# Layer 0 of a two-layer diffusion trunk: when the attention heads' rows are turned, and where the experts' row numbers are made

## The chip, the cores and the metric

The kernel runs on one core of a Trainium2 chip. The metric is the device time of one execution in microseconds, the median of several runs. All work is in 32-bit floating point. The core's engines each take their instructions in a fixed order and wait for one another by semaphores: TensorE multiplies matrices into PSUM (eight banks), VectorE, ScalarE and GpSimd do elementwise work, and the queues of SyncE, ScalarE and GpSimd issue transfers.

## The reference, cut to what matters

There are 256 latent tokens and 256 context tokens of width 1024. Layer 0 normalises them, projects them to five groups of 512 columns (u, gate, q, k, v), runs a recurrence (RG-LRU, in two directions) over u and neighbourhood attention over q, k, v, projects both results back, and then runs a mixture of 16 experts. Layer 1 has other mixers and the same experts. The two parts that the change touches are these:

```python
ux, ug, q, k, v = _split(h @ w_in, EVEN_SPLITS)
...
q, k, kc = rms_norm(q, q_g), rms_norm(k, k_g), rms_norm(kc, k_g)   # per head of 64 columns
...
top_v, top_i = lax.top_k(e_logits, MOE_TOP_K)                      # two experts for each token
...
for e in range(MOE_EXPERTS):
    hid = jax.nn.silu(t @ w1[e]) * (t @ w3[e])
    out = out + gate[:, e:e + 1] * (hid @ w2[e])
```

## The kernel before, in words

**Who sets the order.** The program is written with a framework that tracks the dependencies. Its planner gives each engine its order when the program is built: it reckons with its own costs when each instruction's inputs are ready, and of those that are ready it takes the one that stands earliest in the program. The chip then keeps that order, whether the costs were right or not. PSUM banks have tags: four of tag "a" (results of projections), three of tag "b" (short-lived results), one of tag "m". The buffers of one tag are handed out in turn, so the fourth "b" result waits until the first has been read. The context manager `in_order(PE)` ties TensorE's instructions within it to the order of the program.

**Weights.** A stream of 1 MB pieces comes from memory. `chunk` hands out 1024 columns at a time; each chunk is split by `split` into a rounded part (`L339`, ScalarE) and a rest (`L342`, mostly VectorE, some on GpSimd), with four buffers of each kind, and `mm3` does three matmuls for each product (`L348` to `L350`).

**Projections of layer 0.** `proj` runs a projection in four steps, each of one chunk and 24 matmuls, and yields after each. `qk_rows(0)` projects q: after its four steps it copies the four banks of 128 tokens out (`L698`), squares (`L700`), sums by head (`L701`), computes the reciprocal root (`L704`, `rsqrt`), and yields. Then, for each of the four groups of tokens t, it scales the rows (`L709`, VectorE), transposes them with four TensorE transposes into a "b" bank (`L713`), and writes them to `qT` or `kT` (`L716`, ScalarE). `qk_rows(1)` does the same for k, and then v and the gate are projected. `weave` runs these as its main line, and after each yield of it one and a half steps of the recurrence `lru` (gates `L659` to `L668`, then a root `L670` and scans `L672` to `L684`, once for each direction) and one step of the modulation (`L437`).

**Experts of layer 0.** For each expert e: `first` multiplies the gathered tokens by w1 and w3 (24 matmuls each), `second` by w2 (24 matmuls), `hidden` transposes the result between them (`L1589`), and `take` transposes the next expert's tokens (`L1558`). `rows` makes the list of an expert's tokens two experts ahead: a one-hot matrix (`L1507`, VectorE), four small matmuls for the row numbers into one "b" bank (`L1543`), the row numbers (`L1546`), the gather, then four small matmuls for the gates into a second "b" bank (`L1550`) and their sum (`L1551`). The loop runs p1 of e, `hidden(e-1)`, `take(e+1)`, `rows(e+2)`, p3 of e, `second(e-1)`.

Of the kernel before, what the change touches and what calls it, by code (L numbers as in the profile page):

```python
# [13 lines left out]
OP = mybir.AluOpType  # L14
AX = mybir.AxisListType
PE = mybir.EngineType.PE
# [3 lines left out]
D = 1024  # L20
KC = 8
EPS = 1e-6
NE = 16
# [194 lines left out]
def run_all(g):  # L218
    for _ in g:
        pass  # L220
# [8 lines left out]
NP = 2  # L229
# [23 lines left out]
class Trunk:  # L253
# [361 lines left out]
    def even(self, xn):  # L615
        nc, I, F, R = self.nc, self.I, self.F, self.R
        enter = self.enter(0, xn)
        next(enter)
        hT = self.hT
# [72 lines left out]
        def qk_rows(which):  # L692
            banks = [self.bank("a") for _ in range(4)]
            yield from self.proj([("row", banks[t], t, 0, 512) for t in range(4)], hT)
            ss, rs, rows = F.get(4, 8), F.get(4, 8), [nr() for _ in range(4)]
            jr = Ring(F, 1, 512)
            for t in range(4):
                nc.scalar.copy(rows[t], banks[t])  # L698
                j = jr()
                nc.scalar.activation(j, rows[t], AF.Square)  # L700
                nc.vector.tensor_reduce(ss[:, t], j.rearrange("p (h d) -> p h d", h=8), AX.X, OP.add)  # L701
            F.free(jr)
            ssf, rsf = ss.rearrange("p a b -> p (a b)"), rs.rearrange("p a b -> p (a b)")
            nc.vector.tensor_scalar(ssf, ssf, 1.0 / 64, EPS, op0=OP.mult, op1=OP.add)  # L704
            self.rsqrt(rsf, ssf, 32)
            yield
            for t in range(4):
                qn = rows[t].rearrange("p (h d) -> p h d", h=8)
                nc.vector.tensor_tensor(qn, qn, rs[:, t].rearrange("p (h o) -> p h o", o=1).to_broadcast([P, 8, 64]),  # L709
                                        op=OP.mult)  # L710
                tp = self.bank()
                for c in range(4):
                    nc.tensor.transpose(tp[:, c * P:(c + 1) * P], rows[t][:, c * P:(c + 1) * P], self.ident)  # L713
                tv = tp.rearrange("p (c t) -> p c t", c=4)
                ts_ = slice(t * P, (t + 1) * P)
                nc.scalar.activation((kT if which else qT)[:, :, ts_], tv, AF.Copy, scale=self.col("kg" if which else "qg"))  # L716
            F.free(ss, rs)
            yield

        def mains():  # L720
            yield from qk_rows(0)
            yield from qk_rows(1)
            banks = [self.bank("a") for _ in range(4)]
            yield from self.proj([("row", banks[t], t, 0, 512) for t in range(4)], hT)
            self.vr = F.get(4, 512)
            for t in range(4):
                nc.scalar.copy(self.vr[:, t], banks[t])
            self.ugb = [self.bank("a") for _ in range(4)]
            yield from self.proj([("ws", self.ugb[c], c, 0, 512) for c in range(4)], hT)
# [3 lines left out]
        vr, banks = self.vr, self.ugb  # L733
# [12 lines left out]
        gt = Ring(F, 2, 512)  # L746
        R.free(*hT)
        mh, ml = R.get(KC, 512), R.get(KC, 512)
        for c in range(4):
            t = gt()  # L750
# [769 lines left out]
    def experts_rows(self, l, nt, hd, rk, G, VAL, mxi):  # L1520


        nc, I, F, R = self.nc, self.I, self.F, self.R
# [3 lines left out]
        xgR, uR, yR = self.xgR, Ring(F, 2, 512), Ring(F, 2, D)  # L1527
# [9 lines left out]
        def rows(e):  # L1537

            oh = ohR()
            self.one_hot(oh, "iota", rk, e)  # L1540
            tb = self.bank()
            for t in range(nt):
                nc.tensor.matmul(tb[:, 0:2], oh[:, t], self.vi[:, t], start=(t == 0), stop=(t == nt - 1))  # L1543
            ohs[e] = oh
            gt, dst, xg = gtR(), ddR(), xgR()
            nc.vector.tensor_scalar(dst, tb[:, 0:1], tb[:, 1:2], BIG, op0=OP.add, op1=OP.add)  # L1546
            self.gather(hd, xg, dst)
            tg = self.bank()
            for t in range(nt):
                nc.tensor.matmul(tg[:, 0:3], oh[:, t], VAL[:, t, e], start=(t == 0), stop=(t == nt - 1))  # L1550
            nc.vector.tensor_reduce(gt, tg[:, 0:3], AX.X, OP.add)  # L1551
            st[e] = xg, gt, dst

        def turn(b, xg):
# [6 lines left out]
        def take(e):  # L1561

            xh, xl = xs[e] = xhR(), xlR()
            for b in range(2):
                ps = turn(b, st[e][0])
                pv = ps.rearrange("p (k t) -> p k t", k=4)
                nc.scalar.copy(xh[:, 4 * b:4 * b + 4], pv)
                nc.vector.tensor_tensor(xl[:, 4 * b:4 * b + 4], pv, xh[:, 4 * b:4 * b + 4].bitcast(F32),
                                        op=OP.subtract)

        def first(e):

            p1, p3 = self.bank("a"), self.bank("a")
            run_all(self.proj([("row", p1, 0, 0, 512)], xs[e]))
            u = uR()
            nc.scalar.activation(u, p1, AF.Tanh, scale=0.5)
            nc.vector.scalar_tensor_tensor(u, u, 1.0, p1, op0=OP.add, op1=OP.mult)
            yield
            run_all(self.proj([("row", p3, 0, 0, 512)], xs.pop(e)))
            self.lastv = nc.vector.scalar_tensor_tensor(u, u, 0.5, p3, op0=OP.mult, op1=OP.mult)  # L1580
            st[e] = u, *st[e][1:]
            yield

        def hidden(e):

            u = st[e][0]
            ps = self.bank()
            for k in range(4):
                nc.tensor.transpose(ps[:, k * P:(k + 1) * P], u[:, k * P:(k + 1) * P], self.ident)  # L1589
            uh, ul = us[e] = uhR(), ulR()  # L1590
            pv = ps.rearrange("p (k t) -> p k t", k=4)
            nc.scalar.copy(uh, pv)  # L1592
            self.lastv = nc.vector.tensor_tensor(ul, pv, uh.bitcast(F32), op=OP.subtract)

        def second(e):

            _, gt, dst = st.pop(e)
            uh, ul = us.pop(e)
            if e < NE - NP:
                y = yR()  # L1600
            for c in range(2):
                py = self.bank("a")
                run_all(self.piece([("row", py, 0, 0, 512)], (uh, ul), 0, True, True))
                sl = slice(512 * c, 512 * c + 512)
                if e < NE - NP:
                    nc.scalar.activation(y[:, sl], py, AF.Copy, scale=gt)  # L1606
                else:
                    yh, yl = parts[e]
                    nc.scalar.activation(yh[:, sl], py, AF.Copy, scale=gt)
                    self.lastv = nc.vector.scalar_tensor_tensor(yl[:, sl], py, gt, yh[:, sl].bitcast(F32), op0=OP.mult,  # L1610
                                                   op1=OP.subtract)
            if e < NE - NP:
                self.scatter(yd, y, dst)
            else:
                ps = self.bank()
                for t in range(nt):
                    nc.tensor.matmul(ps[:, t * P:(t + 1) * P], ohs[e][:, t], self.identb, start=True, stop=True)
                nc.scalar.copy(smat[e], ps)
# [21 lines left out]
        def back(t, buf=None):  # L1640

            yy[t] = F.get(D) if buf is None else buf
            getattr(nc, BQ).dma_start(yy[t], yd[t * P:(t + 1) * P, :])
# [4 lines left out]
        self.overflow(l, nt, P, (rk, G), mxi, xt, put, uR.bufs[0], yR.bufs[0])  # L1648
        self.ws.add(F.fits(2048))
        self.ws.keep(2, self.end[l])  # L1650
        take(0)
        for e in range(NE + 1):
            f = first(e) if e < NE else iter(())
            next(f, None)
            if e == NE - NP:
                self.pool_share = 0

            if e:
                hidden(e - 1)
            if e + 1 < NE:  # L1660
                take(e + 1)
            if e + 2 < NE:
                rows(e + 2)
            next(f, None)
            if e:
                second(e - 1)
            if e == NE - NP:
                F.free(yR)
                G2 = [F.get(D) for s in range(2)]
                for s in range(2):  # L1670
                    self.mod_row(G2[s], l, 5, s)
                for t in range(nt):
                    back(t, xgR.bufs[1 + t] if t < 2 else None)
        self.pool_share = 2
        F.free(ohR, gtR, ddR, uR)
        if self.early:
# [3 lines left out]
        for t in range(nt):  # L1680
            for c in range(2):
# [3 lines left out]
                for e in (NE - 2, NE - 1):  # L1685
                    for i, part in enumerate(parts[e]):
                        nc.tensor.matmul(ps, smat[e][:, t * P:(t + 1) * P], part[:, sl], start=False,
                                         stop=(e == NE - 1 and i == 1))
                nc.vector.tensor_tensor(tmp, ps, G2[t // 2][:, sl], op=OP.mult)
                (nc.gpsimd if c == 0 and t < 3 else nc.vector).tensor_tensor(self.x(t)[:, sl], self.x(t)[:, sl], tmp, op=OP.add)  # L1690
# [4 lines left out]
    def experts_sum(self, l, nt, H, rk, rs, G, VAL, mxi):  # L1695
# [4 lines left out]
        for t in range(nt):  # L1700
            nc.scalar.dma_start(self.out[t * P:(t + 1) * P, :], self.x(t))
        G2 = F.get(512)
        for c in range(2):
# [351 lines left out]
```

## Time and profile before

| | |
|---|---|
| time, median of 3 runs | 1212.52 us (1209.02 to 1212.96) |
| profiled execution, own time | 1213.93 us |
| its span, first to last instruction | 1212.1 us |
| mean granted TensorE clock | 0.964 of full speed |
| TensorE busy | 1084.2 us, 89% of the span |
| VectorE busy | 787.8 us, 65% |
| ScalarE busy | 521.0 us, 43% |
| GpSimd busy | 358.4 us, 30% |
| moved by DMA | 317.80 MB, mean 262 GB/s |

Shares are averages over stages with different limits. What a stage is worth is read from its own rows: which wait ends last there.

### The profile page before, as it was taken

What the parts mean: (1) busy time and instruction counts of PE and PEld (TensorE: products, weight loads), DVE (VectorE), ACT (ScalarE), POOL (GpSimd) and SP (SyncE); (2) the same over time, 40 slices, a digit from 0 to 9 for tenths busy, and PEclk for the clock granted to TensorE, in tenths of its full rate; (3) what the DMA queues carried; (4) which work ended last, traced back from release to release, by engine and by line L of the source; (5) the groups of instructions that cost most, each with busy time, mean ns of one, the idle gap of its engine ahead of it and who ended that gap; (6) DMA issues with size and microseconds to landing.
All of it is one profiled execution on the core that took longest, in us unless ns stands there. A gap on an engine that the chain in (4) does not pass through costs nothing. (4 is left out here: it accounts for less than half of the span.)

```text
span 1212.1 us, 17259 instructions
## 1 busy us (share of the span) xinstructions
PE 1084.2 (89%) x6474; PEld 767.5 (63%) x6474; DVE 787.8 (65%) x1373; ACT 521.0 (43%) x803; POOL 358.4 (30%) x227
## 2 busy tenths in 40 slices
PE   3998979999859999999999897988899879999985
PEld 1666656566737777777778555656677756666552
DVE  2576747665557999999989767698748852222111
ACT  2355633443336878787788433433245210000000
POOL 1331414233312445444441222143342501111111
PEclk9999989899989999999999998997999989999998
DMA  9673356456557999999997615332257799999995
GB/s 352 224 231 125 126 174 222 163 210 229 205 148 251 352 342 362 354 363 355 348 361 259 237 61 192 122 139 70 77 174 281 289 408 411 410 420 414 410 416 199
DMA packets 76321, 317.80 MB, mean 262 GB/s; under 512 B 21269, under 2 KB 27533, under 8 KB 47430
## 3 DMA queue, kind: packets, MB, share of 16 engines
q1 hardware_dynamic: 54656, 294.63, 63.4%
q0 software_dynamic: 6912, 11.25, 4.4%
q10 hardware_dynamic: 14662, 10.73, 3.1%
q8 instruction: 54, 0.88, 0.3%
q14 instruction: 37, 0.30, 0.1%
HBM read 309.43 MB, written 17.92 MB: 270 GB/s over the span
## 5 line engine op out<-in xcount | busy, mean ns | idle before, releaser
L339 ACT CAST arena_rw<-arena_f 128x1024 fp32r<-128x1024 f32 x256 | 264.8, 1049 | 174.4 <-PE b L350 96.3
L342 DVE TENSOR_TENSOR arena_rw<-arena_f,arena_rw 128x1024 fp32r<-128x1024 f32 x198 | 254.0, 1322 | 68.3 <-ACT arena_rw L339 67.7
L348 PE MATMUL b<-arena_rw,arena_rr 128*128 128x512 f32 (+1 forms) x736 | 275.5, 375 | 1.8 <-ACT arena_rr L1592 0.8
L349 PE MATMUL b<-arena_rw,arena_rr 128*128 128x512 f32 (+1 forms) x736 | 272.5, 371 | 0.0
L350 PE MATMUL b<-arena_rw,arena_rr 128*128 128x512 f32 (+1 forms) x736 | 270.8, 370 | 1.2 <-DVE arena_rr L1246 1.2
L342 POOL TENSOR_TENSOR arena_rw<-arena_f,arena_rw 128x1024 fp32r<-128x1024 f32 x58 | 145.0, 2502 | 229.8 <-ACT arena_rw L339 217.5
L348 PEld LDWEIGHTS b<-arena_rw,arena_rr 128*128 128x128 f32 x736 | 138.9, 189 | 36.8 <-issue 9.0
L350 PEld LDWEIGHTS b<-arena_rw,arena_rr 128*128 128x128 f32 x736 | 138.2, 189 | 27.8 <-issue 2.8
L349 PEld LDWEIGHTS b<-arena_rw,arena_rr 128*128 128x128 f32 x736 | 139.0, 189 | 23.6 <-issue 1.3
L1761 ACT ACTIVATE arena_f<-b 128x256 f32<-128x256 f32 x16 | 6.1, 384 | 195.0 <-PE b L1754 195.0
L1516 POOL DMA_INDIRECT out<-arena_f x16 | 24.9, 1555 | 211.7 <-DVE arena_f L1787 207.8
L1754 PE MATMUL b<-arena_f 128*64 128x256 f32 x672 | 77.9, 381 | 4.0 <-DMA arena_f<-in_moe 4.0
L437 PE MATMUL b<-arena_f,cs 128*32 128x256 f32 x768 | 67.1, 405 | 16.1 <-DMA arena_f<-in_modw 15.8
L348 PE MATMUL b<-arena_rr,arena_rw 128*128 128x512 f32 (+1 forms) x192 | 74.7, 394 | 2.9 <-ACT arena_f L893 1.5
L350 PE MATMUL b<-arena_rr,arena_rw 128*128 128x512 f32 (+1 forms) x192 | 73.3, 386 | 4.4 <-DVE arena_rw L342 4.4
L349 PE MATMUL b<-arena_rr,arena_rw 128*128 128x512 f32 (+1 forms) x192 | 72.9, 380 | 1.0 <-POOL arena_rr L537 1.0
L1754 PEld LDWEIGHTS b<-arena_f 128*64 128x64 f32 x672 | 47.8, 137 | 31.8 <-issue 6.7
L437 PEld LDWEIGHTS b<-arena_f,cs 128*32 128x32 f32 x768 | 21.4, 111 | 49.1 <-issue 27.8
L348 PEld LDWEIGHTS b<-arena_rr,arena_rw 128*128 128x128 f32 x192 | 36.9, 194 | 18.7 <-issue 7.4
L1787 DVE SCALAR_TENSOR_TENSOR arena_f<-b,arena_f 128x512 f32<-128x512 f32 x16 | 12.0, 751 | 54.7 <-PE b L1782 54.7
L1516 POOL DMA_INDIRECT yd<-arena_f x14 | 32.0, 2283 | 52.0 <-ACT arena_f L1606 52.0
L584 POOL TENSOR_TENSOR arena_f<-arena_f 128x512 f32<-128x512 f32 x21 | 29.6, 1415 | 54.1 <-DVE arena_f L581 52.0
(380 smaller groups left out, 1705.1 us busy)
## 6 DMA issues: line engine op xcount, KB each, us to landing
arena_f<-in_moe SPq DMA_DIRECT2D x192, 1024.0 KB
arena_f<-in_modw SPq DMA_DIRECT2D x96, 512.0 KB
arena_f<-in_wod SPq DMA_DIRECT2D x18, 1024.0 KB
arena_f<-in_wev SPq DMA_DIRECT2D x14, 1024.0 KB
arena_f<-md ACTq DMA_DIRECT2D x8, 512.0 KB
arena_f<-in_tok SPq DMA_DIRECT2D x4, 512.0 KB
yd<-arena_f SPq DMA_DIRECT2D x4, 512.0 KB
arena_f<-yd SPq DMA_DIRECT2D x4, 512.0 KB
```

Of the source, the lines that this page charges most:

```text
L339: nc.scalar.copy(h, raw)
L342: eng.tensor_tensor(l, raw, h.bitcast(F32), op=OP.subtract)
L348: nc.tensor.matmul(ps, ah, bh, start=first, stop=False)
L349: nc.tensor.matmul(ps, ah, bl, start=False, stop=False)
L350: nc.tensor.matmul(ps, al, bh, start=False, stop=last)
L437: nc.tensor.matmul(acc[32 * i:32 * i + 32, 0:256], self.cs[:, k, :], raw[:, i * 256:(i + 1) * 256], start=(k == 0), stop=(k == KC - 1))
L584: (nc.vector if last and c == 3 else nc.gpsimd).tensor_tensor(xs, xs, tmp, op=OP.add)
L1516: self.nc.gpsimd.indirect_dma_start(out=yd[:, :], out_offset=bass.IndirectOffsetOnAxis(ap=dst, axis=0), in_=y, in_offset=None, bounds_chec ...
L1754: nc.tensor.matmul(p[64 * c:64 * c + 64, 0:256], x[:, 4 * b + k], raw[:, 512 * k + 256 * c:512 * k + 256 * c + 256], start=(b == 0 and k = ...
L1761: nc.scalar.activation(u, ps[0], AF.Tanh, scale=0.5)
L1787: nc.vector.scalar_tensor_tensor(y, py, gt, G2, op0=OP.mult, op1=OP.mult)
```

## The change

It has two parts, both in layer 0.

First, `qk_rows` ends after the statistics. The scaling, the transposes and the writing of the turned rows move into `qk_norm(which, ts)`, which a new wrapper `behind` calls from within the following projection: two groups of tokens after its third step, two after its fourth. q's rows are so turned within k's projection, and k's within v's. The main line of `weave` has 22 yields instead of 20.

Second, `rows` puts the row numbers and the gates of an expert into one bank of tag "m", one right after the other, instead of two banks of tag "b", and the loop over the experts stands under `in_order(PE)`.

```diff
@@ qk_rows
             ss, rs, rows = F.get(4, 8), F.get(4, 8), [nr() for _ in range(4)]
+            qk[which] = ss, rs, rows
...
             self.rsqrt(rsf, ssf, 32)
             yield
-            for t in range(4):
+
+        def qk_norm(which, ts):
+
+            ss, rs, rows = qk[which]
+            for t in ts:
                 qn = rows[t].rearrange("p (h d) -> p h d", h=8)
...
-            F.free(ss, rs)
-            yield
+            if 3 in ts:
+                F.free(ss, rs)
+
+        def behind(main, which):
+
+            for i in range(2):
+                next(main)
+                yield
+            for i in range(2):
+                next(main)
+                yield
+                qk_norm(which, (2 * i, 2 * i + 1))
+                yield
+            yield from main
+
+        qk = {}
 
         def mains():
             yield from qk_rows(0)
-            yield from qk_rows(1)
+            yield from behind(qk_rows(1), 0)
             banks = [self.bank("a") for _ in range(4)]
-            yield from self.proj([("row", banks[t], t, 0, 512) for t in range(4)], hT)
+            yield from behind(self.proj([("row", banks[t], t, 0, 512) for t in range(4)], hT), 1)
@@ rows
-            tb = self.bank()
+            tb = self.bank("m")
             for t in range(nt):
                 nc.tensor.matmul(tb[:, 0:2], oh[:, t], self.vi[:, t], start=(t == 0), stop=(t == nt - 1))
+            for t in range(nt):
+                nc.tensor.matmul(tb[:, 2:5], oh[:, t], VAL[:, t, e], start=(t == 0), stop=(t == nt - 1))
...
-            tg = self.bank()
-            for t in range(nt):
-                nc.tensor.matmul(tg[:, 0:3], oh[:, t], VAL[:, t, e], start=(t == 0), stop=(t == nt - 1))
-            nc.vector.tensor_reduce(gt, tg[:, 0:3], AX.X, OP.add)
+            nc.vector.tensor_reduce(gt, tb[:, 2:5], AX.X, OP.add)
@@ experts_rows
-        take(0)
-        for e in range(NE + 1):
...
+        with self.in_order(PE):
+            take(0)
+            for e in range(NE + 1):
...
```

## Rows read from the trace of the kernel before

**Rows 1.** Page, VectorE's costliest group: busy us, mean ns | idle before, releaser.

```profile
L342 DVE TENSOR_TENSOR arena_rw<-arena_f,arena_rw 128x1024 fp32r<-128x1024 f32 x198 | 254.0, 1322 | 68.3 <-ACT arena_rw L339 67.7
```

**Rows 2.** Stretches: busy us of PE, PEld, DVE, ACT, POOL; clock, DMA share, GB/s.

```profile
155.00:205.00 50.00, 40.93 (x195) 30.74 (x195) 26.20 (x38) 17.95 (x23) 13.99 (x6) 0.90 0.64 189
205.00:345.00 140.00, 131.56 (x932) 88.43 (x930) 89.22 (x202) 59.43 (x145) 44.63 (x38) 0.96 0.55 195
...
370.00:650.00 280.00, 269.56 (x1330) 215.43 (x1329) 261.52 (x259) 222.75 (x260) 124.90 (x55) 1.00 0.94 344
```

**Rows 3.** Waits over the whole run: us in total, times, longest.

```profile
PE b L713 <- DVE arena_f L709: 12.7, 2, 9.1
...
PE b L1543 <- DVE arena_rr L1593: 10.4, 13, 1.6
```

**Rows 4.** TensorE around q's transposes: start, us, line, [idle before].

```profile
111.89 0.39 PE L348 MATMUL b<-arena_rw,arena_rr 128*128 128x512 f32 x1
115.90 1.26 PE L713 MATMUL b<-mskt,arena_f 128*128 128x128 f32 x8 [3.63 <-DVE arena_f L709]
...
119.09 1.71 PE L659 MATMUL b<-arena_f 128*128 128x512 f32 x2
```

**Rows 5.** TensorE in order of time around k's transposes.

```profile
154.02 0.50 PE L348 MATMUL b<-arena_rw,arena_rr 128*128 128x512 f32 x1
...
154.83 0.39 PE L348 MATMUL b<-arena_rw,arena_rr 128*128 128x512 f32 x1
164.29 1.12 PE L713 MATMUL b<-mskt,arena_f 128*128 128x128 f32 x4 [9.07 <-DVE arena_f L709]
...
168.58 0.48 PE L349 MATMUL b<-arena_rw,arena_rr 128*128 128x512 f32 x1
```

**Rows 6.** VectorE in order of time, from q's statistics to k's scaling.

```profile
110.84 0.73 DVE L676 TENSOR_TENSOR_SCAN arena_f<-arena_f 128x256 f32<-128x256 f32 x1
...
122.63 0.69 DVE L667 SCALAR_TENSOR_TENSOR arena_f<-arena_f 128x512 f32<-128x512 f32 x1 [4.98 <-ACT arena_f L663]
...
163.55 2.50 DVE L709 TENSOR_TENSOR arena_f<-arena_f 128x512 f32<-128x512 f32 x4
```

**Rows 7.** TensorE through one expert, in order of time.

```profile
503.24 0.60 PE L1589 MATMUL b<-mskt,arena_f 128*128 128x128 f32 x4
503.67 1.04 PE L1558 MATMUL b<-mskt,arena_f 128*128 128x128 f32 x8
504.46 0.48 PE L348 MATMUL b<-arena_rw,arena_rr 128*128 128x512 f32 x1
...
505.49 0.39 PE L349 MATMUL b<-arena_rw,arena_rr 128*128 128x512 f32 x1
506.61 0.24 PE L1543 MATMUL b<-vi,arena_f 128*128 128x2 bf16 x4 [0.73 <-DVE arena_rr L1593]
506.71 0.47 PE L350 MATMUL b<-arena_rw,arena_rr 128*128 128x512 f32 x1
...
507.68 0.39 PE L350 MATMUL b<-arena_rw,arena_rr 128*128 128x512 f32 x1
...
522.62 0.60 PE L1589 MATMUL b<-mskt,arena_f 128*128 128x128 f32 x4
```

**Rows 8.** VectorE through the same expert, in order of time.

```profile
503.11 2.24 DVE L342 TENSOR_TENSOR arena_rw<-arena_f,arena_rw 128x1024 fp32r<-128x1024 f32 x1 [1.10 <-ACT arena_rw L339]
...
507.67 0.21 DVE L1546 TENSOR_SCALAR arena_f<-b 128x1 int32<-128x1 f32 x1
...
522.50 2.26 DVE L342 TENSOR_TENSOR arena_rw<-arena_f,arena_rw 128x1024 fp32r<-128x1024 f32 x1 [1.10 <-ACT arena_rw L339]
```

**Rows 9.** One stretch within the experts of layer 0, columns as in rows 2.

```profile
540.00:560.00 20.00, 19.25 (x96) 15.39 (x95) 18.90 (x19) 15.98 (x19) 9.21 (x6) 1.00 1.00 366
```

**Rows 10.** Waits from 90 to 170 us: us in total, times, longest.

```profile
ACT arena_f L700 <- DVE arena_f L701: 16.9, 4, 9.3
```

**Rows 11.** One stretch within the experts of layer 1, columns as in rows 2.

```profile
1000.00:1060.00 60.00, 60.00 (x490) 38.26 (x488) 17.00 (x47) 3.73 (x10) 6.25 (x4) 1.00 1.02 410
```

More of the change, by code (lines that the diff above doesn't have):

```diff
@@ L1650, in experts_rows @@
         self.ws.keep(2, self.end[l])
-        take(0)
-        for e in range(NE + 1):
[L1653 to L1673, printed above, removed]
+        with self.in_order(PE):
+            take(0)
+            for e in range(NE + 1):
+                f = first(e) if e < NE else iter(())
+                next(f, None)
+                if e == NE - NP:
+                    self.pool_share = 0
+                if e:
+                    hidden(e - 1)
+                if e + 1 < NE:
+                    take(e + 1)
+                if e + 2 < NE:
+                    rows(e + 2)
+                next(f, None)
+                if e:
+                    second(e - 1)
+                if e == NE - NP:
+                    F.free(yR)
+                    G2 = [F.get(D) for s in range(2)]
+                    for s in range(2):
+                        self.mod_row(G2[s], l, 5, s)
+                    for t in range(nt):
+                        back(t, xgR.bufs[1 + t] if t < 2 else None)
         self.pool_share = 2
```

## The prediction

> **What bounds the kernel now.** I read the page first: TensorE is busy 89% of the span, far ahead of the rest, and VectorE's costliest group is the split of weights, L342, with 254.0 us [rows 1]. A sum over stages says little, so I then took the stretches of layer 0 [rows 2]. From the mixer to the end of the experts TensorE is the busiest engine in each: 131.56 of 140 us after the projections, 269.56 of 280 us in the experts. In the experts VectorE follows closely with 261.52 us. The one weak stretch is 155 to 205 us, where TensorE works 40.93 of 50 us at a mean clock of 0.90.
>
> Third, the waits of TensorE [rows 3]. Two concern the change: 12.7 us in two waits for the scaling of q's and k's rows (L709), and 10.4 us in 13 waits of the row numbers' matmuls (L1543) for VectorE's L1593, the last reader of an older "b" bank. So in both places it is TensorE that stands still in a stage that TensorE sets, and idle time removed there shortens the stage, up to the point where another engine takes over.
>
> **Part one, the heads' rows: what it removes.** In the kernel before, the planner put q's transposes inside step two of k's projection. TensorE begins its last matmul there at 111.89 us and stands still 3.63 us until 115.90 [rows 4]. After it the granted clock is at its lower level: 16 transposes and one matmul take from 115.90 to 119.09, 3.19 us. At the full clock eight transposes take 0.79 us (503.67 to 504.46) [rows 7] and one matmul 0.233 us (64 of them from 507.68 to 522.62 [rows 7]), together 1.81 us; the lower clock costs 1.4 us. First place: 5.0 us.
>
> For k the same happens in v's step three. Four of its 24 matmuls have been issued, from 154.02 to 154.83, then TensorE stands still 9.07 us until 164.29, and 16 transposes and three matmuls take until 168.58, 4.29 us where 2.28 would do [rows 5]. Lower clock: 2.0 us. Second place: 11.1 us. Both together, 16.1 us, are the ceiling of part one.
>
> **What it moves.** No instruction is added or removed: the same 8 scalings, 32 transposes and 8 copies run, and the transfers stay, some a step earlier or later on SyncE's queue; the recurrence and modulation are merely dealt out over 22 yields of the main line. The transposes fall behind steps three and four. q's first row is scaled when TensorE goes on at 115.90, and four take 2.50 us [rows 4, 6], so all are by about 118 even in the old order. k's step two has one matmul left at 112.1 us and step three takes 24 x 0.233 = 5.6, with the recurrence's gates between: it ends at 118 or later. So the first 5.0 us go.
>
> For k the moved transposes alone buy little. Behind step three they follow 20 more matmuls, 20 x 0.233 = 4.7 us. With the first 5.0 us gone, step three ends at 155.06 + 4.7 - 5.0 = 154.8. If VectorE still scaled k's rows at 163.55 [rows 6], TensorE would wait again until 164.29, and all that part one gave would be these 4.7 us: its floor.
>
> But VectorE's chain should move too. In the old order the gates of the second direction (L659) come behind q's transposes, at 119.09 [rows 4], since their "b" banks are handed out after those of the transposes; VectorE meanwhile stands idle 4.98 us until 122.63 for them [rows 6]. In the new program all four gate pairs come ahead of q's "b" banks. What then holds them is the scans of the first direction, the last of which ends at 110.84 + 0.73 = 111.57 [rows 6]. That is 7.5 us earlier than 119.09. Scans, k's statistics and scaling follow this chain, so the first of k's transposes could go at 164.29 - 7.5 = 156.8, 2.0 us after step three ends. I leave this wait in and 1.0 us of lower clock behind it, half way between none and the 2.0 us seen: 5.0 + 11.1 - 3.0 = 13.1 us. The planner's new order on ScalarE and VectorE is not in the trace. Its cost lies between nothing and one wait of 9.3 us, the longest of L700 for L701 [rows 10], on which casts of weights could hang; as chunks are split three ahead I stay near the low end and take 1.1. Part one: 12 us, bounds 4.7 and 16.1.
>
> **Part two, the experts.** One expert takes 522.62 - 503.24 = 19.38 us on TensorE [rows 7]. After the tokens' transposes come five matmuls of p3, then the wait of 0.73 us, then row numbers, two matmuls, gates. From 505.49 to 507.68 there are four large matmuls (0.94 us) and eight small ones; the rest, 1.25 us, is the wait, the changes between kinds and the small ones. In the new order the eight small matmuls directly follow the transposes, in a bank whose reader finished an expert ago; four take 0.10 us (506.61 to 506.71), eight 0.2. Saved: 1.05 us, a period of 18.33. Over the 13 experts with a wait (10.4 us, plus 0.32 each for the changes) and the one without, that is at most 14.7 us.
>
> VectorE limits this. It is idle 1.10 us in the period, from its 503.11 to its 522.50 [rows 8], so it works 18.29 us: both engines would then be full. Some of it is stretched: this L342 takes 2.24 us where the mean of its group is 1.32 [rows 1]. I take 0.75 of 1.05 us for each of the 13, 9.8 us, and 0.7 for the one longer wait among them. Part two: 10.5 us, bounds 0 (below) and 14.7. In the first experts the row numbers of 0 and 1 now follow each other through the single bank, under a microsecond; the gather waits there for the written rows anyway. `in_order` adds nothing on TensorE that the chip's fixed order had not: apart from the row numbers the old order is the program's already.
>
> One rule speaks against this part. Two groups in one bank mean that L1546 can start only after the gates' matmuls, 0.1 us later, and it is followed on VectorE by the splits [rows 8]; 14 times 0.1 is 1.4 us if VectorE binds. The Trainium skill (Perfetto Trace Analysis, Optimizing Tensor Performance) wants independent groups of matmuls to rotate through different banks, so that one is read while the next is written. By that rule alone part two would lose those 1.4 us; by the row of the waits it is the old turn through three banks that costs 10.4 us [rows 3], so I keep 10.5.
>
> **What follows.** Downstream nothing has a clock of its own: TensorE leads until 345 us [rows 2], and the experts of layer 1, where DMA is full at 410 GB/s [rows 11], start their stream when earlier stages free the buffers. Both gains are carried to the end. Sum: 1213.93 - 12 - 10.5 = 1191.4 us. The profiled execution is 1.4 us above the median of the runs, 0.1%; I say 1191.
>
> **Rivals.** (a) VectorE's chain stays where it was, being full with scans and k's statistics; part one gives 4.7: 1213.9 - 15.2 = 1198.7. For it: L709 follows the statistics by rsqrt alone. Against: the idle 4.98 us. Chance 0.15.
>
> (b) VectorE becomes the bound of the experts. GpSimd's splits fall on VectorE's and stretch them more often, as in the row of 2.24 us; each expert gives 0.3 instead of 0.75, part two 4: about 1198. For it: 18.29 us of work. Against: the same collisions are already in those 18.29. Chance 0.10. The Trainium skill (SBUF — State Buffer, Who interferes with whom) says that a VectorE instruction with two SBUF inputs contends with GpSimd reads, which fits that row.
>
> (c) Transfers bound the experts: DMA is at 1.00 of its share at 366 GB/s [rows 9]. Part two gives nothing: 1213.9 - 12 = 1202. Against: in layer 1 the same queue moves 410 [rows 11]. Chance 0.10.
>
> (d) Slower: the gates' pairs, now among k's steps, need two of three "b" banks each, which only ScalarE frees (L662, L663); ScalarE can sit 9.3 us in L700 [rows 10] and TensorE behind it. Three such waits, 27.9 us, more than eat the 22.5: 1219. It decides from three on; in the old trace TensorE never waits so. Chance 0.05.
>
> (e) The planner puts the transposes where they were, or later stages give the time back: no change, 1213. Chance 0.05.
>
> **Numbers.** My forecast has 0.55, and its own range is 1183 (both ceilings: 16.1 + 14.7 = 30.8) to 1197 (three quarters of 22.5). The range reaches to (a), (b) and (c): 1183 to 1203. A run can be told from no change from about 0.3%, 3.6 us. Faster 0.88, a little of (c) and (e) falling within: same 0.06, slower 0.06.
>
> **What would show it.** In the new trace no wait of L713 before q's transposes; one of about 2 us before k's (9 us speaks for (a)), and L659's second direction before 115 us. In the experts no wait at L1543 and a period of 18.5 to 18.7 us on TensorE; if it is over 19, VectorE's idle time tells (b) from (c). The prediction is wrong if TensorE shows a new wait of several microseconds between 100 and 205 us.

## The result, and the profile after

The kernel after takes 1201.99 us in the median of five runs (1194.3 to 1204.0), the kernel before 1212.52 (1208.85 to 1218.4): ratio 0.9899, 95% interval 0.9872 to 0.9927. Faster by 1.0%, where the prediction said 1191 us. The profiled execution took 1201.99 us, its span is 1200.2 us, 11.9 less than before. Where these 11.9 us arise is read from a few instructions that stand in both programs (starts in us; hidden(e) is the first transpose between the two products of expert e):

| | first copy of v | tokens 0 transposed | hidden(0) | hidden(15) | end of layer 0 | first expert weights of layer 1 | span |
|---|---|---|---|---|---|---|---|
| before | 174.98 | 364.55 | 386.00 | 668.98 | 688.78 | 922.51 | 1212.1 |
| after | 168.35 | 362.72 | 384.55 | 661.33 | 681.78 | 911.48 | 1200.2 |
| difference | -6.6 | -1.8 | -1.5 | -7.7 | -7.0 | -11.0 | -11.9 |

So the heads' rows gave 6.6 us and not 12; most of that was lost again where the experts begin; the loop gave 6.2 and not 10.5; and 4 us came in layer 1, where nothing was changed.

**Heads' rows.** TensorE in order of time, in the kernel after, around q's and k's transposes (now L718):

```profile
126.23 0.64 PE L437 MATMUL b<-arena_f,cs 128*32 128x256 f32 x8
126.81 1.21 PE L718 MATMUL b<-mskt,arena_f 128*128 128x128 f32 x8
...
155.48 0.64 PE L437 MATMUL b<-arena_f,cs 128*32 128x256 f32 x8
163.22 1.97 PE L718 MATMUL b<-mskt,arena_f 128*128 128x128 f32 x8 [7.10 <-DVE arena_f L714]
```

q's transposes follow without a wait; the 3.63 us of [rows 4] are gone. k's still wait 7.10 us, against 9.07 in [rows 5]: k's scaling, now L714, starts at 162.47 where it started at 163.55 [rows 6]. The scans did move (the last one from 153.97 to 147.85), so something between scans and scaling is late. ScalarE and then VectorE in that stretch, in order of time (ACTq: a transfer issued by ScalarE):

```profile
137.25 1.11 ACT L699 COPY arena_f<-b 128x512 f32<-128x512 f32 x2
...
147.85 1.47 ACTq L469 DMA_DIRECT2D mb<-arena_f  x2
...
150.13 1.05 ACT L339 CAST arena_rw<-arena_f 128x1024 fp32r<-128x1024 f32 x1 [10.83 <-POOL arena_f L684]
153.03 0.63 ACT L701 ACTIVATE arena_f<-arena_f 128x512 f32<-128x512 f32 x1 [1.86 <-DMA mb<-arena_f]
...
154.49 0.63 ACT L701 ACTIVATE arena_f<-arena_f 128x512 f32<-128x512 f32 x1 [0.82 <-DVE arena_f L702]
```

```profile
147.85 0.75 DVE L682 TENSOR_TENSOR_SCAN arena_f<-arena_f 128x256 f32<-128x256 f32 x1
151.21 1.23 DVE L342 TENSOR_TENSOR arena_rw<-arena_f,arena_rw 128x1024 fp32r<-128x1024 f32 x1 [2.61 <-ACT arena_rw L339]
153.70 0.69 DVE L702 TENSOR_REDUCE arena_f<-arena_f 128x8 f32<-128x512 f32 x1 [1.26 <-ACT arena_f L701]
...
162.47 2.49 DVE L714 TENSOR_TENSOR arena_f<-arena_f 128x512 f32<-128x512 f32 x4
```

Two rows just ahead of the last scan, of GpSimd and of VectorE:

```profile
144.86 2.81 POOL L342 TENSOR_TENSOR arena_rw<-arena_f,arena_rw 128x1024 fp32r<-128x1024 f32 x1
145.48 2.34 DVE L465 CAST arena_f<-arena_f 64x256 bf16<-64x256 f32 x1
```

k's rows are copied (L699) by 138.4, but the first square (L701) comes at 153.03, and its releaser is the transfer of L469: the one buffer `jr` for squares lies in memory that this transfer of the modulation was reading. The transfer itself is issued on ScalarE's queue only at 147.85, behind VectorE's cast L465, which takes 2.34 us beside a GpSimd split (0.29 us for the same cast at 142.22). Then square and sum (L702) take turns, since there is one buffer. VectorE stands idle 2.61 and 1.26 us meanwhile: it isn't full.

**Where the experts begin.** SyncE, GpSimd and TensorE in the kernel after (SPq: a transfer issued by SyncE; L1863 is the overflow branch):

```profile
352.91 0.35 SPq L161 DMA_DIRECT2D arena_f<-in_moe  x1
353.61 0.34 SPq L161 DMA_DIRECT2D arena_f<-in_moe  x1
...
353.30 1.11 POOL L1530 DMA_INDIRECT arena_f<-hd,arena_f  x1 [9.52 <-SPq L1863]
...
353.64 0.24 PE L1562 MATMUL b<-vi,arena_f 128*128 128x2 bf16 x4 [5.22 <-PEq L1863]
...
362.72 0.66 PE L1576 MATMUL b<-mskt,arena_f 128*128 128x128 f32 x2 [8.74 <-DMA arena_f<-hd,arena_f]
```

In the kernel before, the same instructions of TensorE, SyncE and GpSimd (expert 1's row numbers, the first weight transfer, the first gather):

```profile
353.72 0.24 PE L1543 MATMUL b<-vi,arena_f 128*128 128x2 bf16 x4
...
357.52 0.34 SPq L161 DMA_DIRECT2D arena_f<-in_moe  x1
...
358.27 1.11 POOL L1511 DMA_INDIRECT arena_f<-hd,arena_f  x1 [9.04 <-DMA hd<-arena_f]
```

There these three stood ahead of the branch, and only the second weight transfer (363.00) and the second gather (360.61) behind it; now all stand behind it, and the two weight transfers follow each other within 0.7 us. The tokens of expert 0 are there 9.42 us after their gather; before, with a gather at 358.27, after 6.28.

**The loop.** TensorE through one expert, and then the splits and the one-hot (L1526) on VectorE beside GpSimd's splits:

```profile
480.14 0.60 PE L1607 MATMUL b<-mskt,arena_f 128*128 128x128 f32 x4
480.58 1.04 PE L1576 MATMUL b<-mskt,arena_f 128*128 128x128 f32 x8
481.45 0.24 PE L1562 MATMUL b<-vi,arena_f 128*128 128x2 bf16 x4
481.55 0.24 PE L1564 MATMUL b<-arena_f 128*128 128x3 bf16 x4
499.15 0.60 PE L1607 MATMUL b<-mskt,arena_f 128*128 128x128 f32 x4
```

```profile
497.69 2.75 POOL L342 TENSOR_TENSOR arena_rw<-arena_f,arena_rw 128x1024 fp32r<-128x1024 f32 x1 [1.46 <-ACT arena_rw L339]
...
499.03 2.49 DVE L342 TENSOR_TENSOR arena_rw<-arena_f,arena_rw 128x1024 fp32r<-128x1024 f32 x1 [0.87 <-ACT arena_rw L339]
...
507.91 3.04 POOL L342 TENSOR_TENSOR arena_rw<-arena_f,arena_rw 128x1024 fp32r<-128x1024 f32 x1 [1.75 <-ACT arena_rw L339]
...
509.18 2.32 DVE L1526 TENSOR_TENSOR arena_f<-mskt,arena_f 128x512 bf16<-128x512 f32 x1
```

Row numbers and gates follow the transposes without a wait: the 10.4 us of [rows 3] are gone. But the period is 499.15 - 480.14 = 19.01 us, against 19.38 [rows 7], and a new kind of wait stands in the waits of TensorE's loads from 400 to 620 us:

```profile
PEld b L349 <- DVE arena_rw L342: 8.8, 21, 0.5
...
PEld b L349 <- POOL arena_rw L342: 3.0, 11, 0.3
```

**Layer 1.** The same instructions of the mixer, between two transfers of the out projection's weights, before and after (columns as in [rows 2]):

```profile
835.97:867.20 31.23, 27.76 (x161) 19.43 (x161) 24.86 (x43) 9.61 (x18) 12.63 (x9) 0.87 0.20 65
```

```profile
828.64:856.19 27.55, 23.51 (x157) 16.87 (x155) 25.78 (x43) 9.40 (x18) 12.95 (x9) 1.00 0.22 75
```

3.7 us, with a mean granted clock of 0.87 against 1.00. In the fourteen profiles of this study the stretch takes 31.1 to 31.3 us six times and 27.5 eight times; the change and its two parts alone have 27.5, before 31.2, but so have five kernels built on the change. These 3.7 us are not counted to the change.

### The profile page after: what moved, and what is told of

The parts are those of the page before. It is cut to its first block, busy times and chain, and to the rows that moved or that the text cites. A ratio compares the mean times of both kernels' runs of the same rounds, so it can differ in the third digit from the quotient of the medians.

```text
span 1200.2 us, 17256 instructions
## 1 busy us (share of the span) xinstructions
PE 1084.5 (90%) x6474; PEld 763.5 (64%) x6474; DVE 785.6 (65%) x1373; ACT 523.2 (44%) x803; POOL 363.4 (30%) x227
## 5 line engine op out<-in xcount | busy, mean ns | idle before, releaser
L342 DVE TENSOR_TENSOR arena_rw<-arena_f,arena_rw 128x1024 fp32r<-128x1024 f32 x198 | 258.5, 1346 | 64.6 <-ACT arena_rw L339 64.3
L342 POOL TENSOR_TENSOR arena_rw<-arena_f,arena_rw 128x1024 fp32r<-128x1024 f32 x58 | 155.7, 2685 | 227.3 <-ACT arena_rw L339 201.0
L349 PEld LDWEIGHTS b<-arena_rw,arena_rr 128*128 128x128 f32 x736 | 139.4, 189 | 36.7 <-DVE arena_rw L342 10.7
L1530 POOL DMA_INDIRECT arena_f<-hd,arena_f x16 | 27.4, 1713 | 60.4 <-DVE arena_f L1569 50.4
```

Source lines behind the costliest of these rows:

```text
L342: eng.tensor_tensor(l, raw, h.bitcast(F32), op=OP.subtract)
L349: nc.tensor.matmul(ps, ah, bl, start=False, stop=False)
L1530: self.nc.gpsimd.indirect_dma_start(out=xg, out_offset=None, in_=hd[:, :], in_offset=bass.IndirectOffsetOnAxis(ap=tk, axis=0), bounds_chec ...
```

## The experiments

All are edits of the kernel after where nothing else is said; each ratio is to runs of the kernel before on the same chip, whose medians were 1210.7 to 1212.7.

**The two parts apart.** heads_alone takes the experts' part back, experts_alone the heads' part:

```
-            tb = self.bank("m")
+            tb = self.bank()
...
-        with self.in_order(PE):
```

```
-            yield from behind(qk_rows(1), 0)
+            yield from qk_rows(1)
...
-        def qk_norm(which, ts):
```

> The kernel after with the experts' rows and loop as before: the heads' part alone. Theory A (read from the two traces): this part gives what the copies of v's rows show, 175.0 to 168.4, 6.6 us, because k's statistics on VectorE hardly moved; it is carried to the end, 1212.5 - 6.6 = 1206, and if the stretch of layer 1 with the lower clock also recovers (3.7 us), 1202. The experts' period stays 19.4 us. Theory B (the prediction's size, 12 us): 1200.5.

1205.34 us, ratio 0.9953 (0.9925 to 0.9981). v's copies start at 168.83, 6.2 us earlier, and hidden(0) at 379.25, 6.8 us earlier; the loop keeps 19.4. Theory A.

> The kernel before with the experts' part alone. Theory A (read from the traces): the loop gives 5.9 us (the period goes from 19.40 to 19.0), but 3.7 to 4.8 us are lost where the experts begin, since expert 1's row numbers now come behind the overflow branch and the gathers behind two transfers of weights: 1212.5 - 1 to - 2 = 1210.5 to 1211.5; tokens' first transposes at 367 to 369 us. Theory B: nothing is lost at the beginning and the loop alone counts: 1206.5. Theory C (the prediction's size, 10.5 us): 1202.

1207.08 us, ratio 0.9952 (0.9934 to 0.9970): 5.6 us, more than theory A gave it by time. In the profile its marks are there: tokens 0 at 368.74, 4.2 us later than before; hidden(0) 4.2 later; a period of 19.0; hidden(15) 2.2 us earlier. Most of the rest of its 6.4 us of span is layer 1's stretch of 27.5. So the two parts each give about 0.5% and add up, and of the second one the loop's gain is paid down at its entrance.

**The entrance.** two_banks:

```
-            tb = self.bank("m")
+            tb = self.bank("b" if e < 2 else "m")
```

> The kernel after, but the row numbers of experts 0 and 1 each in a bank of their own; from expert 2 on in the single bank. Theory A: with the single bank expert 1's row numbers could not be issued before expert 0's gates were read, so the planner put them behind the overflow branch and both gathers with them; undone, both stand ahead of the branch, the first gather is issued ahead of the second weight transfer and lands in about 6 us again instead of 9.4, the tokens' first transposes go from 362.7 to about 359, and the end is 3 to 4 us earlier: 1198 to 1199. Theory B (the prediction's): the first gather waits for the written rows anyway; no change, 1202.

1200.03 us, ratio 0.9887 (0.9853 to 0.9921). Expert 1's row numbers go ahead of the branch again (348.76), tokens 0 stand at 358.69, hidden(0) at 379.92 instead of 384.55, and layer 0 ends at 677.17 instead of 681.78: 4.6 us. Of the 4.0 us at the tokens, 1.2 are an earlier start of the gather (352.15 against 353.30) and 2.9 its faster landing. By time it is 2 us less than the kernel after, which the two intervals don't tell apart; its profile has layer 1's stretch at 31.2. Theory A holds for the place. Its reason was then put to the test, since two things had changed at once: the gathers stand closer together, and the second weight transfer comes earlier. late_second takes the second gather away from there:

```
         rows(0)
-        rows(1)
...
             take(0)
+            rows(1)
```

> The kernel after, with expert 1's row numbers (and so the second gather) behind the transposes of expert 0's tokens. Theory A: what costs 3 to 4 us at the start of the experts is that the two gathers are issued within 2.2 us of each other and land together 9.3 to 9.4 us after the first (in six kernels with 2.3 us or more between them it is 5.4 to 6.5); alone, the first lands after 5.4 to 6.5 us, tokens' transposes at about 359 instead of 362.7, hidden values of expert 0 at 381 to 382.5 instead of 384.5. Theory B: the transfers of weights issued ahead of the gathers cost it; 9.3 us stay.

1205.04 us in one run, whose profile has layer 1's stretch at 31.2. Theory A, that the gathers hold each other up, falls: the first gather is alone and still needs 9.06 us. Its SyncE, GpSimd and TensorE:

```profile
353.24 0.34 SPq L161 DMA_DIRECT2D arena_f<-in_moe  x1
...
353.03 1.11 POOL L1530 DMA_INDIRECT arena_f<-hd,arena_f  x1 [9.47 <-SPq L1863]
...
362.09 1.94 PE L1576 MATMUL b<-mskt,arena_f 128*128 128x128 f32 x8 [13.89 <-DMA arena_f<-hd,arena_f]
```

What agrees with all fourteen traces is the second weight transfer: issued 0.2 to 1.2 us after the gather's start (after, late_second, experts_alone, own_squares) the tokens come after 9.1 to 9.4 us; 1.5 us or more behind it (the other ten) after 4.9 to 6.8. The rows of no_pool, below, whose program on SyncE is that of the kernel after, show the other case by chance of timing:

```profile
352.70 1.11 POOL L1530 DMA_INDIRECT arena_f<-hd,arena_f  x1 [7.91 <-SPq L1863]
...
354.22 0.33 SPq L161 DMA_DIRECT2D arena_f<-in_moe  x1
...
358.08 0.66 PE L1576 MATMUL b<-mskt,arena_f 128*128 128x128 f32 x2 [3.48 <-DMA arena_f<-hd,arena_f]
```

That the transfer is the cause is read from these traces; a kernel that moves it alone wasn't run.

**The squares.** own_squares:

```
-        nr = Ring(F, 4, 512)
+        nr, jr = Ring(F, 4, 512), Ring(F, 4, 512)
...
-            jr = Ring(F, 1, 512)
...
-            F.free(jr)
...
-        F.free(nr)
+        F.free(nr, jr)
```

> The kernel after, with four buffers of their own for the squares of the heads' rows instead of one that is taken from memory which the modulation's transfer has just been reading. Theory A: k's statistics hang on that buffer (first square at 153.0, behind the transfer; then square and sum in turn). With buffers of their own the four sums follow the last scan (148.6), the scaling begins at about 155.5 instead of 162.5, TensorE's wait of 7.1 us before k's transposes shrinks below 1 us, v's copies begin at 161 to 162, and the end is 7 us earlier: 1195. Theory B: VectorE is full with scans and statistics whatever the buffer; the scaling stays at 161 or later, no more than 1.5 us: 1200.5 to 1202.

1198.14 us, ratio 0.9884 (0.9852 to 0.9917). In order of time on VectorE, and k's transposes on TensorE:

```profile
147.66 2.46 DVE L701 TENSOR_REDUCE arena_f<-arena_f 128x8 f32<-128x512 f32 x4 [1.95 <-ACT arena_f L700]
...
156.98 2.50 DVE L712 TENSOR_TENSOR arena_f<-arena_f 128x512 f32<-128x512 f32 x4
...
157.73 1.32 PE L716 MATMUL b<-mskt,arena_f 128*128 128x128 f32 x8 [2.48 <-DVE arena_f L712]
```

The four sums follow each other, the scaling starts 5.5 us earlier, the wait is 2.48 instead of 7.10 us and v's copies start at 161.55, 6.8 us earlier. Theory A, though more of the wait is left than the 1 us that it allowed. GpSimd and VectorE between sums and scaling show what was left:

```profile
151.45 2.99 POOL L342 TENSOR_TENSOR arena_rw<-arena_f,arena_rw 128x1024 fp32r<-128x1024 f32 x1 [0.38 <-POOL arena_rw L342]
152.08 2.40 DVE L703 TENSOR_SCALAR arena_f<-arena_f 128x32 f32<-128x32 f32 x1
```

L703, which takes 0.18 us in the kernel before (there L704, at 158.78), takes 2.40 beside a GpSimd split; a split on VectorE ahead of it takes 2.11 instead of 1.2. Nor are the 5.5 us all the buffer's. The last scan ends 2.9 us earlier (145.71 against 148.60), since here the cast L465 ahead of it takes 0.29 us; from there to the end of the sums 5.7 us are saved; 3.1 are lost again up to the scaling. At hidden(0) only 3.6 us of these are left. GpSimd and VectorE of the same kernel show one place where it goes:

```profile
184.10 5.63 POOL L760 TENSOR_TENSOR arena_f<-arena_f,mskt 128x3072 f32<-128x3072 f32 x1 [10.10 <-PE b L350]
...
185.04 5.77 DVE L342 TENSOR_TENSOR arena_rw<-arena_f,arena_rw 128x1024 fp32r<-128x1024 f32 x1 [5.50 <-DMA arena_f<-md]
```

A split that takes 1.23 us runs 5.77 us beside GpSimd's addition of the bias mask; in the kernel after the addition ran while VectorE stood idle.

**Both mends, and the mask on VectorE.** both joins own_squares and two_banks; both_bias has besides:

```
-        nc.gpsimd.tensor_tensor(bv, bv, self.msk("colm")
+        nc.vector.tensor_tensor(bv, bv, self.msk("colm")
```

> The kernel after with both mends: expert 0's and 1's row numbers in banks of their own, and four buffers of their own for the squares. Theory A: the two act in different places and add up. By the traces of the two runs the experts begin 4.6 us earlier by the first and 3.6 by the second: hidden values of expert 0 at 376 to 377, end about 8 us before the kernel after: 1194 (profiled 1193 to 1197, by whether layer 1's mixer runs at the lower clock). Theory B: the first gather hangs on the written rows in both, and only the larger counts: 379 to 380, 1197.5.

1195.31 us, ratio 0.9867 (0.9837 to 0.9896); hidden(0) at 376.88, as theory A has it, which gave 1194.

> As both, and the attention bias' mask is added by VectorE instead of GpSimd. Theory A: with the squares mended, 6.8 us were won at v's copies but 4.5 lost again where VectorE's split of 5.77 us (else 1.23) runs beside GpSimd's addition of 5.63 us. On VectorE the addition fits into its idle 5.5 us ahead of that split: the split takes 1.2 to 3 us, the first scores come at about 191 instead of 195.7, and the end is 4 us before that of both: 1190. Theory B: the addition waits for the bias' transfers, takes over 4 us on VectorE and delays the split just as long: no change against both.

1195.54 us, ratio 0.9865 (0.9837 to 0.9893). On VectorE the addition takes 3.83 us and the split 1.21:

```profile
184.10 3.83 DVE L760 TENSOR_TENSOR arena_f<-arena_f,mskt 128x3072 f32<-128x3072 f32 x1 [4.69 <-DMA arena_f<-in_rpb]
187.86 1.21 DVE L342 TENSOR_TENSOR arena_rw<-arena_f,arena_rw 128x1024 fp32r<-128x1024 f32 x1
```

hidden(0) starts at 372.95, 3.9 us earlier than in both, as theory A wanted; the medians don't show it (runs of both lie from 1193.2 to 1200.1, of both_bias from 1192.2 to 1197.3). Theory A's 1190 was not reached; by time this stays open.

**What bounds the loop.** few_onehot leaves out the one-hot of experts 2 to 15, no_pool all of GpSimd's splits in the experts:

```
-            self.one_hot(oh, "iota", rk, e)
+            if e < 2:
+                self.one_hot(oh, "iota", rk, e)
```

```
-SHARE = 6
+SHARE = 0
```

> The kernel after, with the one-hot rows of experts 2 to 15 left out (the two buffers keep those of experts 0 and 1), so VectorE has one instruction of 1.2 to 2.3 us less per expert; transfers, TensorE's instructions and their order stay. Theory A (VectorE bounds the experts at 19.0 us, idle 0.87): the period falls to TensorE's own work, 18.3 to 18.5, 7 to 9 us over the loop. Theory B (transfers bound them): 19.0 stays. Theory C (the late splits of GpSimd bound them): TensorE's waits for GpSimd stay, 18.7 to 18.9.

> The kernel after, with all splits of weights in the experts on VectorE instead of every sixth on GpSimd. VectorE takes over two to three splits of 1.23 us per expert and loses the collisions, each of which stretches one of its own instructions by about 1.2 us. Theory A (collisions cost as much as GpSimd saves): period 18.5 to 19.1, no waits for GpSimd. Theory B (GpSimd's share is worth its time): VectorE has 2.5 us more, period 20.5 or more, end 20 us or more later.

Both have a period of 18.40 us; one run each, 1188.46 and 1190.42 us. TensorE in few_onehot:

```profile
470.76 0.60 PE L1608 MATMUL b<-mskt,arena_f 128*128 128x128 f32 x4
...
489.16 0.60 PE L1608 MATMUL b<-mskt,arena_f 128*128 128x128 f32 x4
```

So neither the transfers nor TensorE set 19.0; VectorE's work did, although VectorE still stands idle 10.7 of 220 us behind ScalarE's casts (first row below). 18.4 is TensorE's own: in no_pool neither its matmuls nor its loads wait for anything from 400 to 620 us. For no_pool theory A is right in its sense and still too small (it gave 18.5 at best): the collisions cost more than GpSimd's splits save. VectorE is busy 209.27 us in the kernel after and 210.78 in no_pool of the same 220, at the two periods 18.1 and 17.6 us per expert, though in no_pool it does all the splits. VectorE's costliest groups from 400 to 620 us (busy us, mean ns), after and no_pool:

```profile
L342 DVE TENSOR_TENSOR arena_rw<-arena_f,arena_rw 128x1024 fp32r<-128x1024 f32 x117 | 152.1, 1352 | 10.7 <-ACT arena_rw L339 10.7
L1526 DVE TENSOR_TENSOR arena_f<-mskt,arena_f 128x512 bf16<-128x512 f32 x10 | 23.2, 2319 | 0.0
```

```profile
L342 DVE TENSOR_TENSOR arena_rw<-arena_f,arena_rw 128x1024 fp32r<-128x1024 f32 x144 | 169.3, 1219 | 9.2 <-ACT arena_rw L339 7.8
...
L1526 DVE TENSOR_TENSOR arena_f<-mskt,arena_f 128x512 bf16<-128x512 f32 x10 | 6.8, 684 | 0.0
```

The one-hot takes 2319 ns with GpSimd's splits and 684 without. bank_alone drops `with self.in_order(PE):` and keeps the single bank:

> The kernel after without the loop's fixed order on TensorE; row numbers and gates keep their single bank. Theory A (the prediction's: the fixed order adds nothing in the loop): period 19.0 and no waits of the row numbers; expert 2's row numbers come ahead of expert 0's tokens, within 2 us of the kernel after. Theory B: the order is what took the waits away: waits of the row numbers of 0.7 us return and the period is 19.3 or more.

From the fifth expert on the period is 19.0, without waits of the row numbers: theory A in the loop. By time, one run of 1207.88 us, it is not within the 2 us of the kernel after that theory A gave: its profile has layer 1's stretch at 31.2, which is 3.7 of the difference, and about 2 us more arise behind layer 0's experts, from a cause that stays open. (Expert 2's row numbers come ahead of the tokens of expert 0, hidden(0) at 387.16, the first four periods are 18.2 to 18.8, and hidden(15) is at 661.18 against 661.33.) before_no_pool makes the edit of no_pool in the kernel before:

> The kernel before with no splits on GpSimd in the experts, nothing else. Theory A: the 13 waits of the row numbers hung on VectorE's lateness, and VectorE was late because GpSimd's splits stretch its one-hot (2.7 us, 0.68 without) and splits; then the waits shrink without the change of banks and the period is 18.5 to 18.8: end 8 to 12 us earlier, 1201 to 1204. Theory B: the turn through three banks makes the wait whatever VectorE's speed; period 19.2 or more, no more than 3 us: 1208 to 1211.

1200.05 us, ratio 0.9892 (0.9870 to 0.9914). Without any change of banks the waits at L1543 vanish and the period is 519.99 - 501.48 = 18.51 us:

```profile
501.48 0.60 PE L1589 MATMUL b<-mskt,arena_f 128*128 128x128 f32 x4
...
519.99 0.27 PE L1589 MATMUL b<-mskt,arena_f 128*128 128x128 f32 x1
```

One changed number gives as much as the whole change. **All mends together** (both_bias and no_pool):

> The kernel after with every mend that a trace supports: banks of their own for experts 0 and 1, four own buffers for the squares, the mask addition on VectorE, and no splits on GpSimd in the experts. Theory A: the mends act in different stages and add up: period 18.4 instead of 19.0 (13 times 0.6, 8 us) on top of the 1195.5 of the first three: 1187, layer 0's end at 657 to 660. Theory B: in the experts the transfers (0.94 of the DMA engines' time) or TensorE set 18.4 and the early mends only make TensorE wait there: 1190, as with no splits on GpSimd alone.

1184.52 us (1183.41 to 1187.76), ratio 0.9776 (0.9757 to 0.9794): theory A, which gave 1187, by time and by the period of 18.40. Hidden(0) comes at 373.91; layer 0 ends at 663.73, where theory A had 657 to 660. It beats the kernel before by 2.2% and, across chips, the kernel after by 1.2 to 1.5%.

## Why the prediction was right and where it was not

The sign and the mechanisms named held: both removed waits are gone, and both parts alone are faster. The sizes did not: 22.5 us were forecast, 11.9 stand in the profile, 8.2 without layer 1's clock. The time, 1201.99, is inside the stated range of 1183 to 1203 by 1 us and outside the forecast's own, which ended at 1197. That it is inside owes something to luck, since 3.7 us of the profiled gain came by the clock of a stage that the change doesn't touch. Rival (c) hit the number, 1202, and is wrong all the same: with the transfers as they were, few_onehot has a period of 18.40.

**Part one, first place (5.0 us).** Right but for 0.8 us. q's transposes wait no more, the second direction's gates start at 106.55 to 124.42 instead of 119.09 to 127.08, and v's step three ends with a matmul at 155.15 of 0.40 us, where 154.8 was said.

**Part one, second place (8.1 of 11.1 us).** The step that failed is "Scans, k's statistics and scaling follow this chain". The scans followed, by 6.1 us; the scaling moved 1.08 us, the wait left is 7.10 and not 2.0. Rival (a) gave that size (4.7 us; 6.6 measured), but its reason, a full VectorE, is not what happened: own_squares shows that the statistics hung on the buffer of the squares, and its rows that GpSimd's splits stretch VectorE's chain besides. The 9.3 us of ScalarE in [rows 10], which the prediction weighed as a danger for casts, belong to this chain: ScalarE was already waiting in the squares before. They are not the buffer's alone. In the same gap ScalarE's queue issues L469 (150.46, behind VectorE's cast), and own_squares still has 7.96 us there.

**Part two, the loop (0.75 us per expert).** Mis-sized: 0.4 was measured. Rival (b) named the cause, and few_onehot and no_pool show it: VectorE's work, stretched by GpSimd, sets 19.0. The argument against it, that "the same collisions are already in those 18.29", was true and beside the point: once TensorE's wait went, VectorE's work with its collisions was the bound. By the rule in the Trainium skill (SBUF — State Buffer, Who interferes with whom) a VectorE instruction with two SBUF inputs contends with a GpSimd one that reads SBUF; the trace agrees, with 2319 against 684 ns for the one-hot and 5.77 against 1.21 us for a split.

**Part two, its start (under a microsecond).** Wrong: 4.2 us in experts_alone, 4.6 by two_banks. "The gather waits there for the written rows anyway" is true of the gather's start but for 1.2 us, and not of its landing, which costs 2.9 us more (two_banks). Here the rule of the Trainium skill that independent groups rotate through different banks (Perfetto Trace Analysis, Optimizing Tensor Performance) bears on the trace, which goes further than the 1.4 us priced by it: in one bank expert 1's group waited for the readers of expert 0's, and fell behind the branch.

**`in_order` adds nothing.** Right in the loop (bank_alone).

**Carried to the end one to one.** Only in part. In heads_alone the 6.2 us at v's copies are 6.8 at hidden(0) and at hidden(15). In the kernel after, the experts' new start took most of them; of own_squares' 6.8 GpSimd's addition ate a part; layer 1 added 3.7 by its clock.

## What to carry to other kernels

When a wait is moved off the bounding engine, follow the chain behind it through every buffer, also the scratch buffer that one engine fills and another empties, and ask who used its memory last: that is what sets the new start. A second engine that takes a share of the work is worth it only if its instructions don't stretch those of the first; compare the mean of the same instruction with and without it. And where two loops' first turns share a bank, look where the scheduler puts the second: a branch may have come between.

## What the runs showed of the hardware

- Beside GpSimd's splits, a VectorE instruction of 684 ns takes 2319 ns on average; beside an addition of 5.63 us, one of 1.21 us takes 5.77. Instructions with one input are stretched too: a cast of 0.29 us takes 2.34, and one of 0.18 us on 128x32 values takes 2.40 (own_squares), each beside a split of GpSimd. Taking the experts' splits off GpSimd made the kernel before 12 us faster.
- A gather of 128 rows landed, up to the first transposes, in 4.9 to 6.8 us, but in 9.1 to 9.4 where a second weight transfer of 1024 KB was issued on another queue within 1.2 us after its start.
- The same 30 us of layer 1's mixer ran at a mean granted clock of 0.87 or of 1.00, 31.2 or 27.5 us, in profiles of kernels that don't differ there.
